# Context's first feed-forward chunk in full fp32, drawn between the steps of the lead's second product

## The chip, the cores and the metric

The kernel runs on one core of a Trainium2 chip. The metric is the device time of one execution in microseconds (us); lower is better. Times shown are medians of several runs; a profile is one execution recorded instruction by instruction. Engines are called PE (matmul), DVE (vector), ACT (scalar), POOL (GpSimd) and SP (the queue that issues most DMAs).

## The reference

One transformer layer is computed for 128 context tokens and 1024 latent tokens that share their weights: a feed-forward half-step, a mixer (attention and pooling), and a second feed-forward half-step, each with a residual, a layer norm and a modulation. The part that matters here is the first half-step:

```python
def _modulate(x, shift, scale):
    return x * (1.0 + scale) + shift

def _swiglu(h, w1, w2):
    a, b = jnp.split(h @ w1, 2, axis=-1)
    return (jax.nn.silu(a) * b) @ w2

f1 = _swiglu(_modulate(x, sh1, sc1), lw['ffn1_w1'], lw['ffn1_w2'])
x = _layer_norm(ALPHA * x + 0.5 * g1 * f1, lw['ln_g'][0], lw['ln_b'][0])
```

The model width is 1024 and the hidden width 2816. Shift and scale come from products of a condition vector with `w_mod`; context and latent tokens have conditions of their own.

## The kernel before, in words

**Numbers.** Most products are made of three matmuls each (`mm3`, lines 130 to 132): both operands are split into a high and a low part of type fp32r, the high one by a copy on ACT (line 107), the low one by a subtraction on DVE (line 108), and high x high, high x low and low x high are added up in PSUM. `wide` makes such a pair of a weight and `parted` one of an x piece. A plain fp32 matmul needs no split; the kernel uses it for the modulation products of line 224, for the spread of line 169 and for small transposes (line 232).

**The first block's opening.** `ffn` calls `lead` and then `up`. In `lead` the modulation is made chunk by chunk (`mod_head`, of eight chunks; five by PE on line 224, three by DVE on line 214, whose products go into scratch tiles of the `tmp` tag). As soon as chunk kc is there, the latent rows of piece 0 are loaded and modulated (`piece_input`, lines 416 and 417, on ACT at line 402) and split. The latent product is done in the manner of Strassen and Winograd with seven products, A11, A12, S1, S2, S4, S3 and A22, each of four matmul groups per weight pair. The lead does these for four pairs p at once: A11 as chunks 0 to 3 arrive; copies of it into `s1` (line 655); A12 for pairs 0 and 1 as chunks 4 to 7 arrive, then for pairs 2 and 3 (`second`, which adds on line 667 and takes a silu on line 668); then S1, whose weights are differences (`first_sum`, line 711) and whose operands are sums of the two x halves (`sum_operands`, line 457); then the rest, whose operands `next_operand` and `last_operands` make (lines 462 to 473, 738, 752 and 756).

**Context.** `ctx_ffn` is a generator that does the feed-forward of the 128 context tokens in six chunks of the hidden width, five of 512 and one of 256. A chunk of the up product takes 8 weights of 512 KB, each in two steps (value and gate half), then one step for the silu and product, one for transposes, and two for each of the four (at the end two) weights of the down product. Its first half-steps need the modulated context input, `ctx_x`, made from `x_c` in four loads. The generator is drawn by `tick(n)`, n steps at a time. In the first block it is added after the lead, and `up_prod` ticks once after each product of the 18 later pairs, and once more at A12 for pairs below 15 and at S2.

**What sets the order.** The order written is a priority. Before the run a planner that simulates the engines lists each engine's instructions in a fixed order: the ready one of highest priority first, and a tile's buffer is one of those that the pool has free. On the chip each engine, and SP's queue of DMA issues, takes its list strictly in that order. Pools that matter here: `raw`, five buffers of 4 KB a partition, into which SP loads weights (line 111); `tmp`, six buffers of 2 KB; `pc`, twelve of 2 KB; and eight PSUM banks.

Of the kernel before, what the change touches and what calls it, by code (L numbers as in the profile page):

```python
# [26 lines left out]
F32R = mybir.dt.float32r  # L27
# [5 lines left out]
P = 128  # L33
D = 1024
KC = 8
# [12 lines left out]
LAT, CTX = 0, 1  # L48
# [6 lines left out]
class Layer:  # L55
# [417 lines left out]
        self.A["A22"].append(self.parted(r, "b2", 12))  # L473


    def ctx_operands(self):
        place = self.xm if "xm" in self.pools else self.pc
        self.xc = [(place(F32R), place(F32R)) for _ in range(2)]

    def ctx_x(self, x, i, kcs):  # L480
        for kc in kcs:
            m = self.pc()[:, :P]
            self.modulated(m, x[kc], i, CTX, kc)
            ks = slice(kc % 4 * P, (kc % 4 + 1) * P)
            self.split(self.xc[kc // 4][0][:, ks], self.xc[kc // 4][1][:, ks], m)

    def ctx_x_dram(self):
        self.ctx_operands()
        for h in range(2):
            m = self.raw(self.x2_d[0][:, h * 512 : (h + 1) * 512], 512)  # L490
            b = self.bank()
            js = [slice(j * P, (j + 1) * P) for j in range(4)]
            for j in js:
                self.transpose(b[:, j], m[:, j])
            for k, j in enumerate(js):
                self.modulated(m[:, j], b[:, j], 2, CTX, 4 * h + k)
            self.split(self.xc[h][0], self.xc[h][1], m)
            yield

    def ctx_up(self, b, w, kc, n):  # L500
        hi, lo = self.wide(self.raw(w, 2 * n), 2 * n)
        ks = slice(kc % 4 * P, (kc % 4 + 1) * P)
        xh, xl = self.xc[kc // 4]
        for s in range(2):
            ns = slice(s * n, (s + 1) * n)
            self.mm3(b[s][:, :n], (xh[:, ks], xl[:, ks]), (hi[:, ns], lo[:, ns]), kc == 0, kc == KC - 1)
            yield

    def ctx_ffn(self, i, x, w1c, w1t, w2):
        nc = self.nc  # L510
        if x:
            self.ctx_operands()
            x()
        yield
        acc = None
        for c in range(6):
            n = 256 if c == 5 else 512
            banks = [self.bank(), self.bank()]
            for kc in range(KC):
                yield from self.ctx_up(banks, w1t[kc] if c == 5 else w1c[c, kc], kc, n)  # L520
            h = self.tmp() if c == 0 and "xm" in self.pools else self.pc()
            nc.scalar.activation(h[:, :n], banks[0][:, :n], AF.Silu)
            nc.vector.tensor_tensor(h[:, :n], h[:, :n], banks[1][:, :n], ALU.mult)
            yield
            if acc is None:
                acc = [self.bank(), self.bank()]
            b = self.bank()
            for j in range(n // P):
                self.transpose(b[:, j * P : (j + 1) * P], h[:, j * P : (j + 1) * P])
            hh, hl = self.pc(F32R), self.pc(F32R)  # L530
            self.split(hh[:, :n], hl[:, :n], b[:, :n])
            yield
            for j in range(n // P):
                f = 4 * c + j
                js = slice(j * P, (j + 1) * P)
                hi, lo = self.wide(self.raw(w2[f]))
                for d in range(2):
                    ds = slice(d * 512, (d + 1) * 512)
                    self.mm3(acc[d], (hh[:, js], hl[:, js]), (hi[:, ds], lo[:, ds]), f == 0, f == NF - 1)
                    yield  # L540
        for d in range(2):
            o = self.pc()
            nc.scalar.activation(o, acc[d], AF.Copy)
            nc.gpsimd.dma_start(self.fc_d[i][:, d * 512 : (d + 1) * 512], o)
            yield
# [34 lines left out]
    def up_pair(self, m, w1, h_d):  # L580

        nc = self.nc
        add, sub = (partial(nc.vector.tensor_tensor, op=o) for o in (ALU.add, ALU.subtract))
        halves = lambda t: (t[:, :512], t[:, 512:])
        ra, rb = self.raw(w1[2 * m]), self.raw(w1[2 * m + 1])
        (b11, b21), (b12, b22) = halves(ra), halves(rb)
        hi, lo = self.wide(ra)
        Y = self.bank()
        self.up_prod(Y, "A11", (hi[:, :512], lo[:, :512]), True)
        s1 = self.tmp()  # L590
        nc.scalar.activation(s1, Y, AF.Copy)
        yield
        t = self.tsum()
        sub(t[:, 0, :], b12, b11)
        sub(t[:, 1, :], b22, t[:, 0, :])
        t12 = self.wide(self.flat(t))
        Z = self.bank()
        self.up_prod(Z, "A12", (hi[:, 512:], lo[:, 512:]), True, 1 + self.spare * (m < 15))
        add(s1, Z, s1)
        nc.scalar.activation(s1, s1, AF.Silu)  # L600
        yield
        w22 = self.wide(b22, 512)
        X = self.bank()
        self.up_prod(X, "S1", [halves(w)[0] for w in t12], True)
        s5 = self.tmp()
        nc.scalar.activation(s5, X, AF.Copy)
        yield
        sub(b11, t[:, 1, :], b11)
        sub(b21, b21, t[:, 1, :])
        t34 = self.wide(ra)  # L610
        self.up_prod(Y, "S2", [halves(w)[1] for w in t12], False, 1 + self.spare)
        u2 = self.tmp()
        nc.scalar.activation(u2, Y, AF.Copy)
        yield
        self.up_prod(X, "S4", w22, False)
        add(u2, X, u2)
        nc.vector.tensor_tensor(u2, u2, s1, ALU.mult)
        self.keep_h(m, 0, u2, h_d)
        yield
        self.up_prod(Y, "S3", [halves(w)[0] for w in t34], False)  # L620
        add(s5, Y, s5)
        yield
        self.up_prod(Y, "A22", [halves(w)[1] for w in t34], False)
        sa = self.tmp()
        nc.scalar.activation(sa, Y, AF.Silu)
        nc.vector.tensor_tensor(s5, s5, sa, ALU.mult)  # L626
        self.keep_h(m, 1, s5, h_d)
        self.h_sums(m, u2, s5, h_d)
        yield
# [20 lines left out]
    def lead(self, w1, h_d, piece, make, Y=None):  # L650


        nc = self.nc
# [18 lines left out]
        if not begun:  # L672
# [9 lines left out]
            s1 = [self.tmp() for p in R]  # L682
            for p in R:
                copy(s1[p], Y[p])
            Z = [self.bank() for p in range(2)]
            for k in range(4):
                if k < 3:
                    ready(5 + k)
                if k >= 2:
                    S += [self.sum_operands(piece, j) for j in (2 * k - 4, 2 * k - 3)]  # L690
                for p in range(2):
                    self.up_unit(Z[p], "A12", W2[p], k, k == 0, k == 3)
            for p in R:
                second(p, Z[p] if p < 2 else self.bank(), p >= 2)
        else:
            W2 = [self.wide(part(0, p, 1), 512) for p in R]
            s1 = [self.tmp() for p in R]
# [32 lines left out]
        else:  # L730
            for p in R:
                first_sum(p)
                X.append(self.bank())
                prod(X[p], "S1", self.wide(T[p], 512), True)
                self.next_operand(p, *S[p])
        for p in R:
            r = part(1, p, 1)
# [12 lines left out]
        for p in R:  # L750
            r = part(0, p, 0)
            sub(r, T[p], r)
            prod(Y[p], "S3", self.wide(r, 512), False)
            add(s5[p], Y[p], s5[p])
            r = part(0, p, 1)
            sub(r, r, T[p])
            prod(Y[p], "A22", self.wide(r, 512), False)
            sa = self.tmp()
            nc.scalar.activation(sa, Y[p], AF.Silu)
            nc.vector.tensor_tensor(s5[p], s5[p], sa, ALU.mult)  # L760
            self.keep_h(p, 1, s5[p], h_d)
            if begun and p == 0:
                self.tick(5)

    def up(self, w1, h_d):
# [220 lines left out]
    def ffn(self, i, head, res_of, dst, order, half, beside=None, begun=None):  # L986
# [3 lines left out]
        with ExitStack() as st:  # L990
# [10 lines left out]
                self.begin_operands()  # L1001
            piece, make, ctx_x, mods = head()
            context = self.ctx_ffn(i // 2, ctx_x, a["w1c_" + s], a["w1t_" + s], a["w2_" + s])
            if begun:
                self.add_side(context)
            self.lead(a["w1_" + s], h_d, piece, make, Y)
            self.mods = mods
            if not begun:
                self.add_side(context)
            self.up(a["w1_" + s], h_d)  # L1010
            self.flush()
            for _ in self.mods:
# [8 lines left out]

    def head_input(self):
        nc, a = self.nc, self.a

        def ctx_x():
            for q in range(4):
                x = self.pc()
                nc.sync.dma_start(x[:, :256], a["x_c"][q])
                self.ctx_x({q: x[:, :P], q + 4: x[:, P:256]}, 0, (q, q + 4))

        def mods():
            for part in range(2, 5):
                yield from self.mod_part(part)
# [10 lines left out]
            if kc == 0:  # L1044
                self.spread(1, rows[2:])

        return self.piece_input, make, ctx_x, mods()

    def head_dram(self):
        return self.piece_dram, lambda kc: None, None, self.mod_part(8)  # L1050
# [536 lines left out]
def _layout(inputs):  # L1587
# [32 lines left out]
    for i, w in enumerate(WINDOWS):  # L1620
# [3 lines left out]
    return {  # L1624
        "x": con(x),
        "x_l": con(x[P:].T.reshape(KC, P, 2, 512).transpose(2, 0, 1, 3)[::-1]),
        "x_c": con(x[:P].T.reshape(2, 4, P, P).transpose(1, 2, 0, 3)).reshape(4, P, 256),
        "w_mod": con(wm_t[16:]),
        "w_mod_v": con(np.stack([np.stack([wm_t[k], wm_t[KC + k]]) for k in DVE_KC])),
        "w_mod_h": con(  # L1630
# [53 lines left out]
```

## Time and profile before

| what | value |
|---|---|
| median of 3 runs | 2496.45 us (2493.36 to 2497.18) |
| the profiled execution, its own time | 2495.49 us |
| span of the profile | 2493.7 us |
| PE busy | 2452.3 us, 98% of the span |
| DVE busy | 1830.6 us, 73% |
| ACT busy | 1214.5 us, 49% |
| moved by DMA | 463.75 MB, mean 186 GB/s |

A profile's row of a group reads: line, engine, operation, output tile and input tiles, partitions by elements and type, how many times, then busy time and mean ns of one, then the idle time of the engine just before and what released it. A row of the order in time begins with the start and the length in us; `x4` means four instructions merged into one row. The ends of matmuls are modelled and overlap with the next start, so the distance from one start to the next is what one costs. In a view of stretches each engine has its busy us with the number of instructions behind it, and then come the granted PE clock as a share of full speed, the share of DMA time and GB/s.

The lead lies in the first 125 us or so; the up stage follows until about 557 us, where the context's result is stored.

### The profile page before, as it was taken

The page shows a single profiled execution, that of the slowest core. Times are in us where ns is not written, and L with a number is a line of the kernel's source. Part 1 is how long each engine was busy: PE and PEld are TensorE (multiplying, and loading weights), DVE is VectorE, ACT ScalarE, POOL GpSimd, SP SyncE. Part 2 cuts the span into 40 slices and gives each one's busy share as a digit, 9 for nine tenths or more (in the row PEclk, how much of TensorE's full clock was granted, in tenths as well). Part 3 has the DMA queues.
Part 4 walks back from the last instruction along what each step waited for, and adds up shares of the span by engine and source line. Part 5 has one row for each costly group of instructions (what it writes and reads, how often), then busy time and mean ns, then how long its engine had stood idle before and what let it go on. Part 6 is the DMA issues. An engine that isn't in the chain of part 4 may idle for free.

```text
span 2493.7 us, 34226 instructions
## 1 busy us (share of the span) xinstructions
PE 2452.3 (98%) x12297; PEld 2115.0 (85%) x12297; DVE 1830.6 (73%) x2817; ACT 1214.5 (49%) x2094; POOL 463.4 (19%) x691
## 2 busy tenths in 40 slices
PE   8999999999999999999999999999899999999998
PEld 4788888888889989889999999998688888887887
DVE  6877778877678556566888886876877666676877
ACT  5544444444445343434778773435744344444442
POOL 0000011110022212232567640110000001111002
PEclk9999999999999999999999999999999999999999
DMA  7455566778686555534100035665754445558773
GB/s 292 144 167 188 182 224 230 244 259 326 213 276 218 184 180 189 188 136 163 42 1 2 1 110 187 237 215 185 223 173 164 150 173 195 205 197 320 269 267 121
DMA packets 167554, 463.75 MB, mean 186 GB/s; under 512 B 18900, under 2 KB 37636, under 8 KB 167384
## 3 DMA queue, kind: packets, MB, share of 16 engines
q1 hardware_dynamic: 140952, 373.79, 44.7%
q0 software_dynamic: 23696, 86.32, 9.3%
q8 instruction: 97, 1.59, 0.3%
q10 hardware_dynamic: 2736, 1.44, 0.2%
q14 instruction: 73, 0.60, 0.1%
HBM read 390.42 MB, written 71.07 MB: 185 GB/s over the span
## 4 chain that ended last, share of the span: by engine, by line
PE 84%; DVE 6%; issue 4%; DMA 3%; ACT 2%; POOL 1%; SPq 0%; DVEq 0%; POOLq 0%; ACTq 0%
PE w L130 24%; PE w L131 24%; PE w L132 24%; PE w L1060 8%; PE w L135 3%; DVE op L108 1%; DVE x L108 1%; DMA raw<-w 1%; DVE mx L1389 1%; PE w L224 0%; DMA yc<-fc 0%; ACT pr L1397 0%; DMA raw<-w1c 0%; DVE so L108 0%; DMA raw<-x 0%
## 5 line engine op out<-in xcount | busy, mean ns | idle before, releaser
L107 ACT ACTIVATE op<-raw 128x1024 fp32r<-128x1024 f32 (+1 forms) x505 | 483.9, 969 | 517.4 <-PE w L131 263.4
L108 DVE TENSOR_TENSOR op<-raw,op 128x1024 fp32r<-128x1024 f32 (+1 forms) x505 | 558.9, 1116 | 233.1 <-ACT op L107 201.1
L130 PE MATMUL w<-b,op 128*128 128x512 f32 x880 | 343.9, 393 | 7.1 <-ACT b L107 2.9
L131 PE MATMUL w<-b,op 128*128 128x512 f32 x880 | 344.6, 392 | 0.0
L132 PE MATMUL w<-b,op 128*128 128x512 f32 x880 | 339.7, 391 | 0.3 <-DVE op L108 0.3
L130 PE MATMUL w<-x,op 128*128 128x384 f32 x768 | 260.0, 339 | 0.0
L131 PE MATMUL w<-x,op 128*128 128x384 f32 x768 | 258.8, 337 | 0.0
L132 PE MATMUL w<-x,op 128*128 128x384 f32 x768 | 257.7, 337 | 0.0
L131 PE MATMUL w<-op,so 128*128 128x512 f32 (+1 forms) x627 | 242.4, 387 | 2.0 <-DVE op L108 2.0
L132 PE MATMUL w<-op,so 128*128 128x512 f32 (+1 forms) x627 | 241.9, 387 | 0.0
L130 PE MATMUL w<-op,so 128*128 128x512 f32 (+1 forms) x627 | 232.7, 386 | 1.0 <-ACT op L107 0.9
L130 PEld LDWEIGHTS w<-b,op 128*128 128x128 f32 x880 | 165.6, 188 | 42.9 <-ACT b L107 3.4
L562 POOL DMA_DIRECT2D h<-tmp x80 | 43.4, 543 | 851.6 <-DVE tmp L626 426.1
L132 PEld LDWEIGHTS w<-b,op 128*128 128x128 f32 x880 | 165.8, 188 | 35.8 <-DVE op L108 0.8
L131 PEld LDWEIGHTS w<-b,op 128*128 128x128 f32 x880 | 165.8, 188 | 34.8 <-DVE b L108 0.7
L1402 POOL TENSOR_TENSOR pr<-pr,sm 128x384 f32<-128x384 f32 x192 | 156.1, 842 | 95.1 <-DVE sm L1400 71.8
L190 DVE SCALAR_TENSOR_TENSOR junk<-raw,sil 128x1024 bf16<-128x1024 f32 x112 | 135.9, 1224 | 26.0 <-DMA raw<-w_mod 25.6
L107 ACT ACTIVATE so<-sr 128x1024 fp32r<-128x1024 f32 (+1 forms) x84 | 82.7, 986 | 136.1 <-PE w L131 82.7
L131 PEld LDWEIGHTS w<-x,op 128*128 128x128 f32 x768 | 144.1, 188 | 0.3
L130 PEld LDWEIGHTS w<-x,op 128*128 128x128 f32 x768 | 144.1, 188 | 0.4
L132 PEld LDWEIGHTS w<-x,op 128*128 128x128 f32 x768 | 143.9, 188 | 0.0
L131 PEld LDWEIGHTS w<-op,so 128*128 128x128 f32 x627 | 118.2, 189 | 26.8 <-DVE op L108 3.2
(323 smaller groups left out, 5136.6 us busy)
## 6 DMA issues: line engine op xcount, KB each, us to landing
raw<-w SPq DMA_DIRECT2D x240, 256.0 KB, 5.3
raw<-w SPq DMA_DIRECT2D x116, 512.0 KB, 3.9
raw<-w1c SPq DMA_DIRECT2D x80, 512.0 KB, 4.0
sr<-h SPq DMA_DIRECT2D x70, 512.0 KB, 5.7
raw<-w_mod SPq DMA_DIRECT2D x56, 512.0 KB, 4.3
raw<-w_gate SPq DMA_DIRECT2D x48, 512.0 KB, 3.7
h<-tmp POOLq DMA_DIRECT2D x80, 256.0 KB, 3.6
h<-pc POOLq DMA_DIRECT2D x52, 256.0 KB, 4.6
```

Source lines behind the costliest of these rows:

```text
L107: self.nc.scalar.activation(hi, src, AF.Copy)
L108: self.nc.vector.tensor_tensor(lo, src, hi.bitcast(F32), ALU.subtract)
L130: mm(out, lhsT=lh, rhs=rh, start=start, stop=False)
L131: mm(out, lhsT=lh, rhs=rl, start=False, stop=False)
L132: mm(out, lhsT=ll, rhs=rh, start=False, stop=stop)
L135: self.nc.tensor.transpose(out, src, self.ident)
L190: nc.vector.scalar_tensor_tensor(junk, w, 1.0, self.sil[cond], ALU.mult, ALU.mult, accum_out=self.mod[:, cond, b : b + 1],)
L562: self.nc.gpsimd.dma_start(h_d[f // 2][:, 2 * kh + n, f % 2, :], h)
L1060: self.nc.tensor.matmul(acc[h][j], lhsT=lhs[:, part, js], rhs=w[wi][:, h * 512 : (h + 1) * 512], start=f, stop=l)
L1389: nc.vector.tensor_reduce(mx[:, c : c + 1], b[:, :GT], AX.X, ALU.max)
L1402: nc.gpsimd.tensor_tensor(pr[:, c, :], pr[:, c, :], sm[:, 3:4].broadcast_to([P, GT]), ALU.mult)
```

## The change

In the first block the context generator is added before the lead, and the lead draws it. Chunk 0 of its up product no longer uses split operands: `ctx_whole_input` loads all of the context input into two `tmp` tiles with one tick ahead of A12; each weight's two steps then modulate one 128x128 part of it in place and do one plain fp32 matmul each, straight from the loaded weight. Four such steps follow each of the four matmul groups of A12 for pair 0. A12 of pairs 1 to 3 comes whole afterwards, each followed by the `sum_operands` of one index, which came earlier before. The S1 weights are split for all four pairs ahead of the S1 products, with one tick (the silu of chunk 0) between. Five ticks now also come at A22 of pair 0 in the first block. Chunk 1 and later chunks use the split context input as before; it is made at chunk 1's start from a second load of `x_c` (`ctx_parts_input`). The extra ticks in `up_prod` become fewer. `x_c` lies in memory as two blocks of 512 columns and no longer as four of 256. The second block's work is the same as before.

```diff
+    def ctx_whole_input(self):
+        self.xf = [self.tmp() for _ in range(2)]
+        for h, x in enumerate(self.xf):
+            self.nc.sync.dma_start(x, self.a["x_c"][h])
+
+    def ctx_parts_input(self):
+        self.xc = [(self.pc(F32R), self.pc(F32R)) for _ in range(2)]
+        for h in range(2):
+            m = self.pc()
+            self.nc.sync.dma_start(m, self.a["x_c"][h])
+            for k in range(4):
+                js = slice(k * P, (k + 1) * P)
+                self.modulated(m[:, js], m[:, js], 0, CTX, 4 * h + k)
+            self.split(self.xc[h][0], self.xc[h][1], m)
...
-    def ctx_up(self, b, w, kc, n):
+    def ctx_up(self, b, w, kc, n, whole):
+        ks = slice(kc % 4 * P, (kc % 4 + 1) * P)
+        if whole:
+            x = self.xf[kc // 4][:, ks]
+            self.modulated(x, x, 0, CTX, kc)
+            r = self.raw(w, 2 * n)
+            for s in range(2):
+                self.nc.tensor.matmul(
+                    b[s][:, :n], lhsT=x, rhs=r[:, s * n : (s + 1) * n],
+                    start=kc == 0, stop=kc == KC - 1,
+                )
+                yield
+            return
         hi, lo = self.wide(self.raw(w, 2 * n), 2 * n)
...
             banks = [self.bank(), self.bank()]
+            if x and c == 1:
+                x[1]()
             for kc in range(KC):
-                yield from self.ctx_up(banks, w1t[kc] if c == 5 else w1c[c, kc], kc, n)
+                yield from self.ctx_up(banks, w1t[kc] if c == 5 else w1c[c, kc], kc, n, x and c == 0)
-            h = self.tmp() if c == 0 and "xm" in self.pools else self.pc()
+            h = self.tmp() if c == 0 else self.pc()
...
-        self.up_prod(Z, "A12", (hi[:, 512:], lo[:, 512:]), True, 1 + self.spare * (m < 15))
+        self.up_prod(Z, "A12", (hi[:, 512:], lo[:, 512:]), True, 1 + self.spare * (m < 10))
...
-        self.up_prod(Y, "S2", [halves(w)[1] for w in t12], False, 1 + self.spare)
+        self.up_prod(Y, "S2", [halves(w)[1] for w in t12], False)
...
-            Z = [self.bank() for p in range(2)]
+            Z = self.bank()
             for k in range(4):
                 if k < 3:
                     ready(5 + k)
-                if k >= 2:
-                    S += [self.sum_operands(piece, j) for j in (2 * k - 4, 2 * k - 3)]
-                for p in range(2):
-                    self.up_unit(Z[p], "A12", W2[p], k, k == 0, k == 3)
+                if k == 0:
+                    self.tick(1)
+                self.up_unit(Z, "A12", W2[0], k, k == 0, k == 3)
+                self.tick(4)
             for p in R:
-                second(p, Z[p] if p < 2 else self.bank(), p >= 2)
+                second(p, self.bank() if p else Z, p > 0)
+                S.append(self.sum_operands(piece, p))
...
             for p in R:
                 first_sum(p)
+            W = [self.wide(T[p], 512) for p in R]
+            self.tick(1)
+            for p in R:
                 X.append(self.bank())
-                prod(X[p], "S1", self.wide(T[p], 512), True)
+                prod(X[p], "S1", W[p], True)
                 self.next_operand(p, *S[p])
...
-            if begun and p == 0:
+            if p == 0:
                 self.tick(5)
...
-            if begun:
-                self.add_side(context)
+            self.add_side(context)
             self.lead(a["w1_" + s], h_d, piece, make, Y)
             self.mods = mods
-            if not begun:
-                self.add_side(context)
```

More of the change, by code (lines that the diff above doesn't have):

```diff
@@ L473, in last_operands @@
         self.A["A22"].append(self.parted(r, "b2", 12))
[L476 to L485, printed above, removed]
+    def ctx_whole_input(self):
[11 more added lines that the diff above has]
+            self.split(self.xc[h][0], self.xc[h][1], m)
     def ctx_x_dram(self):
-        self.ctx_operands()
+        self.xc = [(self.xm(F32R), self.xm(F32R)) for _ in range(2)]
         for h in range(2):
@@ L498, in ctx_x_dram @@
             yield
-    def ctx_up(self, b, w, kc, n):
+    def ctx_up(self, b, w, kc, n, whole):
[11 more added lines that the diff above has]
+            return
         hi, lo = self.wide(self.raw(w, 2 * n), 2 * n)
-        ks = slice(kc % 4 * P, (kc % 4 + 1) * P)
         xh, xl = self.xc[kc // 4]
@@ L511, in ctx_ffn @@
         if x:
-            self.ctx_operands()
-            x()
+            x[0]()
         yield
@@ L1023, in head_input @@
         nc, a = self.nc, self.a
[L1025 to L1029, printed above, removed]
         def mods():
@@ L1045, in make @@
                 self.spread(1, rows[2:])
-        return self.piece_input, make, ctx_x, mods()
+        return self.piece_input, make, (self.ctx_whole_input, self.ctx_parts_input), mods()
     def head_dram(self):
@@ L1626, in _layout @@
         "x_l": con(x[P:].T.reshape(KC, P, 2, 512).transpose(2, 0, 1, 3)[::-1]),
-        "x_c": con(x[:P].T.reshape(2, 4, P, P).transpose(1, 2, 0, 3)).reshape(4, P, 256),
+        "x_c": con(x[:P].T.reshape(2, 4, P, P).transpose(0, 2, 1, 3)).reshape(2, P, 512),
         "w_mod": con(wm_t[16:]),
```

## The prediction

> **What bounds the kernel now.** I read the page's totals first, then the stretches of the opening and of the up stage, then the TensorE (PE) instructions in order of time.
>
> ```profile
> span 2493.7 us, 34226 instructions
> PE 2452.3 (98%) x12297; PEld 2115.0 (85%) x12297; DVE 1830.6 (73%) x2817; ACT 1214.5 (49%) x2094; POOL 463.4 (19%) x691
> ```
>
> ```profile
> 40.00:45.00 5.00, 5.00 (x24) 3.34 (x23) 2.21 (x8) 3.79 (x7) 0.00 (x0) 1.00 1.05 386
> 45.00:50.00 5.00, 4.73 (x22) 2.28 (x21) 5.00 (x16) 5.00 (x9) 0.00 (x0) 1.00 0.53 195
> ...
> 100.00:150.00 50.00, 50.00 (x222) 41.39 (x222) 33.34 (x45) 17.59 (x23) 3.78 (x7) 1.00 0.46 156
> ```
>
> ```profile
> 50.00:55.00 5.00, 4.79 (x21) 3.63 (x21) 4.81 (x9) 5.00 (x10) 0.00 (x0) 1.00 0.35 107
> 55.00:60.00 5.00, 3.79 (x17) 2.81 (x16) 5.00 (x10) 3.55 (x7) 0.00 (x0) 1.00 0.35 105
> 60.00:65.00 5.00, 1.39 (x4) 0.37 (x2) 5.00 (x10) 1.30 (x3) 0.00 (x0) 0.84 0.17 54
> 65.00:70.00 5.00, 4.48 (x11) 3.52 (x12) 5.00 (x9) 4.40 (x8) 0.00 (x0) 0.50 0.36 103
> 70.00:75.00 5.00, 5.00 (x23) 4.14 (x22) 5.00 (x10) 5.00 (x11) 0.00 (x0) 0.97 0.17 57
> ```
>
> The columns are PE, weight load, DVE, ACT, POOL, granted clock, DMA share and GB/s. From 100 us on PE is full, so there time is the count of matmuls. From 45 to 70 us PE has a hole while DVE is full, and after it the granted clock is 0.50. The hole's size comes from the matmuls themselves:
>
> ```profile
> 42.47 0.28 PE L232 MATMUL w<-ident,ts 2*128 2x2 f32 x2
> ...
> 44.27 3.62 PE L224 MATMUL w<-wm,silt 128*2 128x256 f32 x16
> ...
> 58.30 0.50 PE L131 MATMUL w<-ax,op 128*128 128x512 f32 x1 [1.21 <-DVE ax L108]
> ...
> 60.02 0.39 PE L132 MATMUL w<-ax,op 128*128 128x512 f32 x1
> 62.03 0.50 PE L130 MATMUL w<-b,op 128*128 128x512 f32 x1 [1.62 <-ACT op L107]
> 62.51 0.49 PE L131 MATMUL w<-b,op 128*128 128x512 f32 x1
> 65.52 0.79 PE L130 MATMUL w<-b,op 128*128 128x512 f32 x1 [2.52 <-DVE tmp L667]
> ...
> 70.33 0.40 PE L132 MATMUL w<-b,op 128*128 128x512 f32 x1
> 70.57 0.39 PE L130 MATMUL w<-b,op 128*128 128x512 f32 x1
> ...
> 91.89 0.39 PE L130 MATMUL w<-b,op 128*128 128x512 f32 x1
> ```
>
> From 70.57 to 91.89 94 matmuls start: 0.227 us each. From 42.47 to 70.57 (28.1 us) PE runs the 48 matmuls of the second product (A12, four pairs), the modulation product L224 of chunk 7, two small transposes, and 14 matmuls of S1. At full pace that is 62 x 0.227 + 3.6 + 0.4 = 18.1 us, so the hole is 10.0 us: about 4.8 us of waiting between 60.25 and 65.52, 2.3 us because 12 matmuls took 5.05 us at the low clock instead of 2.7, and 3 us in small gaps.
>
> **The change, part by part.** *Removed.* Context's chunk 0 no longer splits its weights; 16 steps of three matmuls leave the full up stage: 48 x 0.227 = **-10.9 us**, one for one, as PE is full there. The eight ACT copies and eight DVE subtractions that go with them were covered by that PE work and count nothing; if a step had waited for its pair it would gain more, but a stretch with 50.00 of 50.00 shows no such wait.
>
> *Added.* 16 full fp32 matmuls, 128x128 by 128x512, among the A12 of pair 0. The trace has none of that size; the nearest rows:
>
> ```profile
> L224 PE MATMUL w<-wm,silt 128*2 128x256 f32 x80 | 22.5, 445 | 0.2 <-DMA wm<-w_mod_h 0.2
> ```
>
> ```profile
> 14.15 0.18 PEld L169 LDWEIGHTS w<-pc,ones 1*128 1x128 f32 x1 [0.24 <-issue]
> 14.58 0.18 PEld L169 LDWEIGHTS w<-pc,ones 1*128 1x128 f32 x1 [0.24 <-issue]
> ```
>
> Each fp32 matmul is two PE instructions (eight written in L224 for one chunk, x16 in the row at 44.27). There 16 passes of 256 columns take 3.62 us, 0.226 each, so 0.45 for 512; the 512-column passes of L169 load 0.43 apart. A step is 0.86 to 0.91 us; I take 0.88, between two near ends: **+14.1 us** (13.8 to 14.5).
>
> *Where that lands.* Hole 10.0 us, fill 14.1: if the steps fill it, S1, which now runs as if from 70.57 - 14 x 0.227 = 67.4 us without a break, starts at 42.47 + 10.9 + 3.6 + 0.4 + 14.1 = 71.5. The lead is 4.1 us longer, and the whole is 4.1 - 10.9 = **-6.8 us** before new stalls. The steps need no split, so they depend only on DMA and on a 128x128 modulation each (eight; ACT):
>
> ```profile
> L402 ACT ACTIVATE pc<-pc,md 128x128 f32<-128x128 f32 x8 | 3.8, 488 | 3.9 <-DMA pc<-x_c 3.9
> ...
> L711 DVE TENSOR_TENSOR ts<-raw 128x512 f32<-128x512 f32 x4 | 2.7, 684 | 0.0
> ```
>
> Eight of 0.49 us are 3.9 us on ACT, in place of eight 512-wide modulations of the second x piece that come later; nothing on PE waits for them but the steps.
>
> *DMA and SP's queue.* Eight loads of 512 KB and two of 256 KB (4.7 MB) now stand ahead of these:
>
> ```profile
> 28.47 0.33 SPq L416 DMA_DIRECT2D xp<-x_l  x1
> 29.75 8.81 SPq L416 DMA_DIRECT2D pc<-x_l  x8
> 38.90 32.92 SPq L111 DMA_DIRECT2D raw<-w  x17
> ```
>
> ```profile
> pc<-x_l SPq DMA_DIRECT2D x12, 256.0 KB, 8.2
> ```
>
> At 386 GB/s they take 12.2 us. The eight pieces of x's second half, landed by about 46 now (the last issue at 29.75 + 8.81 - 0.33 = 38.2, and 8.2 to land), land by 59. The raw pool has five buffers, so the sixth to eighth weight must wait on SP until PE finished steps 2, 4 and 6 (about 46 to 53 us), with x and the first_sum halves queued behind: first pair by 51 to 56, last by 59 to 61. DVE still owes S1 four adds, four splits, four subtractions L711, four splits of these and four L667: 20 x 0.69 = 13.8 us, from about 56 to 70, against S1 at 71.5. That fits with little to spare. The stall has ends of 0 (all ordered well) and 9 us (next part); the margin is on the lower end's side, and I take **2 us**: -4.8 us.
>
> What such a stall costs depends on the clock. The gap of 1.21 us at 58.30 was followed by matmuls at the full pace; the stretch from 60.25 to 65.52, with two matmuls in it, by 12 at half, at 2.3 us. A stall of 2 us lies between these, nearer to the first, so I add nothing; with the drop the sum is -2.5. The Trainium skill ("TensorE: Matmul & The Clock Gate", section "What's actually happening") states that the clock halves after an idle window of about 3.4 us. This trace agrees on both sides, 1.21 and 4.8 us; by it a 2 us stall stays free of the drop and the sum is -4.8 too.
>
> *Costed at nothing.* The number of steps drawn stays 155: before 18 x 7 + 11 + 18, after 1 + 16 + 1 + 5 in the lead and 18 x 7 + 6, so nothing piles up in the flush. The later x_c load and its eight modulations and two splits at chunk 1 (8 x 0.49 + 2 x 0.69 = 5.3 us of ACT and DVE) lie under the full PE; if a step of chunk 1 had to wait for them, that is the price. The five ticks put two weight splits into the lead, on DVE, after S1.
>
> **The rivals.** *DVE's run only moves back.* Its order is fixed before the run; what S1 needs may again stand behind the S2 and S4 operands.
>
> ```profile
> 45.41 0.69 DVE L457 TENSOR_TENSOR pc<-pc,pc 128x512 f32<-128x512 f32 x1
> ...
> 64.78 2.48 DVE L667 TENSOR_TENSOR tmp<-w,tmp 128x512 f32<-128x512 f32 x4
> ```
>
> Now S1 comes 67.4 - 45.4 = 22 us after the first add. From a first add at 56 that makes 78; with 2.3 us of low clock, 80.5: a stall of 9 us and a net of +2.2: 2498.6. For it speaks that L667 ran at 64.78 although the products ended by 60.4. Against it: the adds of the second half now stand behind L667 in the order written, and fewer can be ahead of it.
>
> *Slower: the six tmp buffers.* Four hold s1 and two the context input, so none is left for chunk 6's products on DVE, whose scratch has the same tag.
>
> ```profile
> 41.22 2.07 ACT L655 ACTIVATE tmp<-w 128x512 f32<-128x512 f32 x4 [3.03 <-PE w L132]
> ```
>
> ```profile
> 37.31 1.22 DVE L214 SCALAR_TENSOR_TENSOR junk<-wm,sil 128x1024 bf16<-128x1024 f32 x1
> ...
> 43.06 1.22 DVE L214 SCALAR_TENSOR_TENSOR junk<-wm,sil 128x1024 bf16<-128x1024 f32 x1
> ...
> 46.09 1.22 DVE L214 SCALAR_TENSOR_TENSOR junk<-wm,sil 128x1024 bf16<-128x1024 f32 x1
> ```
>
> If they wait for the first input half, freed after step 8 (42.5 + 3.6 + 6 x 0.227 + 8 x 0.88 = 54.5), DVE stands in its queue till then, four products take 4.9 us, and A12's third part starts at about 62. If DVE's 22 us then begin, S1 starts at 84: a stall of 12.5 us, +5.7: 2502. It decides from a stall of 11.8 us. Against it: the first of the four ran ahead of the copies at 37.31, and the steps that remain can run meanwhile.
>
> *More gain.* No stall at all, and fewer steps per pair ease DVE in the up stage. PE's idle time there is about 1 us, so -6.8 becomes about -8: 2488.5.
>
> That the steps run in one block and are not spread changes PE's sum by nothing; it is in the first two cases.
>
> **How the numbers follow.** The profiled execution took 2495.49 us around its span of 2493.7; the median of the runs is 2496.45, 1 us above. The differences are taken from the median. A measurement here tells 0.2%, 5 us, from no change. Forecast, stall 0 to 4 us (-6.8 to -2.8): 0.50, at -4.8 = **2491.6**. DVE's run moved back: 0.22. Tmp buffers: 0.16. More gain: 0.12. The forecast is under -5 for stalls below 1.8 us, 0.30 of its 0.50. Faster 0.30 + 0.12 = 0.42; same 0.20 + 0.22 = 0.42; slower 0.16. The range reaches from the last case's far side to the tmp case: 2487 to 2502.5; the forecast's own is 2489.6 to 2493.7.
>
> **What would show it.** The step as pairs of fp32 passes at 0.43 to 0.455 us; PE without a gap over 2 us between 42 and 72 and the clock at 1.00 there; S1 from 71 to 74 us; 48 fewer matmuls with pc operands in the up stage, whose end comes 3 to 7 us earlier. It would be wrong if S1 starts after 78, if junk or x_l on the queues waits for a buffer past 55, or if the up stage does not shrink by about 11 us.

## The result, and the profile after

The changed kernel takes 2509.74 us in the median of 6 runs (2506.03 to 2510.59), against 2495.96 us for 6 runs of the kernel before (2493.36 to 2497.18). The ratio is 1.0054, 95% interval 1.0043 to 1.0064: slower by 13.8 us. The forecast was 2491.6, with a range up to 2502.5.

The profiled execution is longer by 11.8 us of span. From the page of the changed kernel:

```profile
span 2505.5 us, 34175 instructions
PE 2458.9 (98%) x12281; PEld 2113.4 (84%) x12281; DVE 1822.6 (73%) x2803; ACT 1208.7 (48%) x2088; POOL 461.9 (18%) x691
```

The context's sum is read back for the first norm at 642.4 us before and 654.7 us after, 12.3 us later; from there to the end the distance stays between 10 and 12.5 us (11.8 at the same read-back of the second block). So all of it is lost ahead of that, and the stretches of the opening show where (columns as in the prediction: PE, weight load, DVE, ACT, POOL, granted clock, DMA share, GB/s):

```profile
45.00:50.00 5.00, 0.73 (x2) 0.30 (x2) 3.53 (x7) 4.69 (x8) 0.00 (x0) 0.61 0.85 333
50.00:55.00 5.00, 3.40 (x4) 1.17 (x4) 2.40 (x4) 2.94 (x7) 0.00 (x0) 0.50 0.01 4
55.00:60.00 5.00, 5.00 (x19) 1.80 (x19) 0.00 (x0) 0.37 (x1) 0.00 (x0) 0.87 0.30 105
60.00:65.00 5.00, 5.00 (x13) 2.14 (x12) 0.16 (x1) 0.00 (x0) 0.00 (x0) 1.00 0.47 137
...
70.00:75.00 5.00, 1.62 (x6) 1.05 (x6) 5.00 (x15) 3.98 (x7) 0.00 (x0) 1.00 0.73 238
75.00:80.00 5.00, 3.42 (x5) 1.52 (x6) 5.00 (x10) 5.00 (x10) 0.00 (x0) 0.68 0.61 194
80.00:85.00 5.00, 5.00 (x18) 3.16 (x17) 5.00 (x10) 0.67 (x2) 0.00 (x0) 0.98 0.64 207
```

PE stands still at 45 to 51 and again after 68, and DVE, which was full here before, does nothing from 55 to 64 us. The PE instructions in order of time (L511 is the fp32 step):

```profile
42.25 0.28 PE L232 MATMUL w<-ident,ts 2*128 2x2 f32 x2
...
45.54 0.40 PE L132 MATMUL w<-ax,op 128*128 128x512 f32 x1
51.60 3.78 PE L511 MATMUL w<-raw,tmp 128*128 128x512 f32 x4 [5.67 <-ACT tmp L402]
55.31 4.09 PE L224 MATMUL w<-wm,silt 128*2 128x256 f32 x16
59.33 8.85 PE L511 MATMUL w<-raw,tmp 128*128 128x512 f32 x20
68.11 0.28 PE L232 MATMUL w<-ident,ts 2*128 2x2 f32 x2
71.83 0.47 PE L130 MATMUL w<-ax,op 128*128 128x512 f32 x1 [3.44 <-DVE md L202]
72.14 0.40 PE L131 MATMUL w<-ax,op 128*128 128x512 f32 x1
72.38 0.39 PE L132 MATMUL w<-ax,op 128*128 128x512 f32 x1
...
73.07 0.39 PE L132 MATMUL w<-ax,op 128*128 128x512 f32 x1
76.58 1.07 PE L130 MATMUL w<-ax,op 128*128 128x512 f32 x2 [3.13 <-ACT ax L107]
77.49 5.03 PE L511 MATMUL w<-raw,tmp 128*128 128x512 f32 x8
81.95 0.80 PE L131 MATMUL w<-ax,op 128*128 128x512 f32 x1
82.59 0.39 PE L132 MATMUL w<-ax,op 128*128 128x512 f32 x1
```

A pass is one of the two PE instructions of an fp32 matmul. Twenty passes start within 59.33 to 68.0: 0.434 us each, 0.87 a step, as the prediction had it. From 42.25 to 82.59 (40.3 us; PE is full after it) the work is 15 A12 matmuls x 0.227, 32 passes x 0.434, 3.6 for L224 and 0.4 for the small transposes: 21.3 us. The hole is 19.0 us, where it was 10.0. With the 16 steps at +13.9 and the 48 matmuls at -10.9 the sum is +3.0 + 9.0 = +12.0, against 11.8 in the spans. The price of the work was right; the hole doubled instead of closing.

Two other engines tell what PE waited for. SP's queue:

```profile
30.40 9.44 SPq L416 DMA_DIRECT2D pc<-x_l  x8
40.19 2.37 SPq L111 DMA_DIRECT2D raw<-w1c  x4
42.91 1.00 SPq L479 DMA_DIRECT2D tmp<-x_c  x2
55.41 7.97 SPq L111 DMA_DIRECT2D raw<-w1c  x3
64.78 60.44 SPq L111 DMA_DIRECT2D raw<-w  x27
```

and DVE:

```profile
51.74 0.69 DVE L108 TENSOR_TENSOR b<-xp,b 128x512 fp32r<-128x512 f32 x1
64.84 1.22 DVE L214 SCALAR_TENSOR_TENSOR junk<-wm,sil 128x1024 bf16<-128x1024 f32 x1 [12.41 <-issue]
```

The context input x_c is issued at 42.91, behind all of x's second half and five of the weights (one went ahead at 23.31), though its tick is written ahead of them; so the first step can't start before 51.60. And DVE waits 12.4 us in front of chunk 6's scratch. The row names no releaser. But that scratch and the context input share the `tmp` tag, and the scratch started at 64.84, when step 8, the last reader of the input's first half, was done (four passes by 55.3 and twelve from 59.33: 59.33 + 12 x 0.434 = 64.5).

### The profile page after: what moved, and what is told of

Read it like the earlier page. It is cut to its first block, busy times and chain, and to the rows that moved or that the text cites. A ratio compares the mean times of both kernels' runs of the same rounds, so it can differ in the third digit from the quotient of the medians.

```text
span 2505.5 us, 34175 instructions
## 1 busy us (share of the span) xinstructions
PE 2458.9 (98%) x12281; PEld 2113.4 (84%) x12281; DVE 1822.6 (73%) x2803; ACT 1208.7 (48%) x2088; POOL 461.9 (18%) x691
## 4 chain that ended last, share of the span: by engine, by line
PE 90%; DVE 5%; ACT 2%; DMA 2%; issue 1%; POOL 0%; SPq 0%; DVEq 0%; POOLq 0%; ACTq 0%
PE w L130 26%; PE w L131 26%; PE w L132 26%; PE w L1071 8%; PE w L135 3%; DMA raw<-w 1%; PE w L224 1%; DVE x L108 1%; DVE op L108 1%; DVE mx L1400 1%; PE w L511 1%; ACT pr L1408 0%; ACT pc L402 0%; DVE pl L1333 0%; ACT b L107 0%
## 5 line engine op out<-in xcount | busy, mean ns | idle before, releaser
L107 ACT ACTIVATE op<-raw 128x1024 fp32r<-128x1024 f32 (+1 forms) x497 | 475.0, 967 | 523.6 <-PE w L131 266.9
L108 DVE TENSOR_TENSOR op<-raw,op 128x1024 fp32r<-128x1024 f32 (+1 forms) x497 | 548.6, 1113 | 220.3 <-ACT op L107 182.5
L107 ACT ACTIVATE so<-sr 128x1024 fp32r<-128x1024 f32 (+1 forms) x84 | 82.7, 986 | 136.9 <-PE w L131 70.4
L130 PE MATMUL w<-ax,op 128*128 128x512 f32 x352 | 138.2, 399 | 9.1 <-ACT ax L107 5.7
```

Of the source, the lines that this page charges most:

```text
L107: self.nc.scalar.activation(hi, src, AF.Copy)
L108: self.nc.vector.tensor_tensor(lo, src, hi.bitcast(F32), ALU.subtract)
L130: mm(out, lhsT=lh, rhs=rh, start=start, stop=False)
```

## The experiments

In the tables of a trace some lines move by one where an edit adds a line; the fp32 step is then L512, the latent modulation L403.

**The two waits, one at a time and together.** `xf_mid` loads the context input earlier:

```diff
                     W2 = [self.wide(part(0, p, 1), 512) for p in R]
+                    self.tick(1)
                 for p in R:
...
-                if k == 0:
-                    self.tick(1)
                 self.up_unit(Z, "A12", W2[0], k, k == 0, k == 3)
```

> The changed kernel, with the one tick that loads the context input moved into the A11 loop (at chunk 2, behind the second weights). The two tmp tiles are then taken before the scratch of chunk 4, and x_c is loaded before the second half of x. Theory 'tmp buffers': two waits make up the loss, the late x_c (PE idle from 45.9 to 51.6 us, then half clock) and chunk 6's scratch waiting for step 8. This run takes away the first only: about 8 us less than the changed kernel, so +3 to +6 us against before. Rival 'queue' (eight 512 KB weights ahead of x's second half and of the first_sum halves on SP): stays at +10 to +14. Rival 'order of DVE' (the sums now late): stays at +10 to +14.

`junk_ts` moves chunk 6's scratch on DVE from `tmp` to the `ts` pool:

```diff
             for part in range(2):
+                wide = self.pools["ts"].tile([P, 2, D], BF16, tag="ts", name=self.name("junk"), bufs=2) if kc == 6 else None
...
-                    junk = self.junk()
+                    junk = self.junk() if wide is None else wide[:, cond, :]
```

> The changed kernel, with chunk 6's scratch on DVE in the ts pool and no longer in tmp. Theory 'tmp buffers': takes away the second wait only (DVE idle from 52.4 to 64.8 us); x_c stays late. PE's waits at 68.1 and 73.3 us go, some 6 to 9 us: +3 to +6 us against before. Rivals 'queue' and 'order of DVE': +9 to +14, as nothing on SP or in the order written has moved.

Both edits:

> Both edits: the early x_c and the scratch in ts. Theory 'tmp buffers': the forecast of the prediction comes about, -3 to -7 us against before. Rival 'queue': +5 or more, since all eight weights still stand ahead of the first_sum halves. Rival 'order of DVE': +3 or more.

And another way to the same end, the input in one buffer of the b2 pool:

```diff
-        self.xf = [self.tmp() for _ in range(2)]
+        t = self.pools["b2"].tile([P, D], F32, tag="b2", name=self.name("xf"), bufs=12)
+        self.xf = [t[:, :512], t[:, 512:]]
```

> The changed kernel, with the whole context input in one buffer of the b2 pool and no longer in two of tmp; the scratch stays in tmp and finds buffers there. Theory 'tmp buffers': the same as both edits together, -3 to -7 us against before, in another way. Rivals 'queue' and 'order of DVE': +3 or more.

Measured, all against the same runs of the kernel before (2495.05 us):

| kernel | median us | ratio, 95% interval | difference us |
|---|---|---|---|
| x_c early | 2496.59 | 1.0006 (0.9996 to 1.0015) | +1.5 |
| scratch in ts | 2506.35 | 1.0043 (1.0028 to 1.0058) | +11.3 |
| both | 2488.61 | 0.9976 (0.9967 to 0.9986) | -6.4 |
| input in b2 | 2489.47 | 0.9975 (0.9964 to 0.9985) | -5.6 |

The kernels without either wait come out faster than the one before, in two ways. That settles it for `tmp`: in both, all eight weights still stand ahead of the first_sum halves, and the sums stand where the new order writes them (with both edits they run from 46.8 to 54.3), so the rivals "queue" (the weights hold up x's second half and the first_sum halves on SP) and "order of DVE" (the sums now stand later) fall as first causes. PE in the kernel with both edits:

```profile
40.67 0.28 PE L233 MATMUL w<-ident,ts 2*128 2x2 f32 x2
40.88 0.50 PE L130 MATMUL w<-ax,op 128*128 128x512 f32 x1
41.22 1.88 PE L512 MATMUL w<-raw,tmp 128*128 128x512 f32 x4
...
51.58 7.03 PE L512 MATMUL w<-raw,tmp 128*128 128x512 f32 x16
58.04 1.03 PE L130 MATMUL w<-ax,op 128*128 128x512 f32 x2
58.91 1.88 PE L512 MATMUL w<-raw,tmp 128*128 128x512 f32 x4
...
61.55 3.60 PE L512 MATMUL w<-raw,tmp 128*128 128x512 f32 x8
...
70.44 0.39 PE L130 MATMUL w<-b,op 128*128 128x512 f32 x1
70.66 0.39 PE L131 MATMUL w<-b,op 128*128 128x512 f32 x1
71.79 0.50 PE L132 MATMUL w<-b,op 128*128 128x512 f32 x1 [0.74 <-DVE op L108]
72.13 0.40 PE L130 MATMUL w<-b,op 128*128 128x512 f32 x1
```

The steps begin at 41.22, S1 at 70.44. From 40.67 to 72.13 (31.5 us) lie 48 A12 and 3 S1 matmuls, 32 passes, L225 and the transposes: 29.5 us, a hole of 2.0. So +3.0 + 2.0 - 10.0 = -5.0, within the interval of the -6.4 measured.

The halves don't add up, and the expectations for them missed: the early load alone gave back 12 us and not 8, the scratch alone only 2, and its +11.3 lies in the range that the two rivals had for it. With x_c early but the scratch in `tmp`, DVE's wait shows its releaser:

```profile
53.69 0.68 DVE L108 TENSOR_TENSOR b<-xp,b 128x512 fp32r<-128x512 f32 x1
57.00 1.22 DVE L214 SCALAR_TENSOR_TENSOR junk<-wm,sil 128x1024 bf16<-128x1024 f32 x1 [2.63 <-PE w L511]
```

It is the fp32 step. PE of the same kernel (the first four passes lie at 42.64):

```profile
51.65 8.74 PE L511 MATMUL w<-raw,tmp 128*128 128x512 f32 x20
63.22 1.22 PE L130 MATMUL w<-ax,op 128*128 128x512 f32 x2 [2.83 <-ACT ax L107]
```

Step 8 is done at 51.65 + 12 x 0.434 = 56.9 and not at 64.5, so DVE's wait has shrunk from 12.4 to 2.6 us; PE still waits 2.8 us for the modulation that follows, and its clock is at half from 63.0 to 69.8. From 42.09 to 70.96, where PE is full again, lie 28.9 us for 21.3 us of work, a hole of 7.6: +3.0 + 7.6 - 10.0 = +0.6, for +1.5 measured.

With x_c late and the scratch out of the way, something else ends at nearly the same time. DVE of `junk_ts`, and then its SP queue:

```profile
53.66 1.28 DVE L469 TENSOR_TENSOR xp<-xp,pc 128x512 f32<-128x512 f32 x2
71.53 0.69 DVE L729 TENSOR_TENSOR ts<-raw 128x512 f32<-128x512 f32 x1 [16.59 <-DMA raw<-w]
```

```profile
42.94 1.00 SPq L480 DMA_DIRECT2D tmp<-x_c  x2
56.24 8.61 SPq L111 DMA_DIRECT2D raw<-w1c  x3
66.24 28.23 SPq L111 DMA_DIRECT2D raw<-w  x17
```

DVE now stands 16.6 us before the first_sum subtraction, whose halves SP issues only behind the last context weights. Those wait for one of the five raw buffers, and the buffers hold weights that no step has read, because the steps wait for x_c. So the rival "queue" was right about a wait, but as something that follows from the late x_c. The hole of this kernel (40.80 to 89.61 us, with 29.7 us of work) is 19.1 us, as large as that of the changed kernel. The late x_c thus reaches DVE in two ways, and taking away one leaves the other.

**Why x_c comes late.** The input in the b2 pool, with its tick where it was, settles that the pool held it back, and not the tick's place in the order written or SP's queue. Its issues (ns shortest/median/longest, first and last start in us):

```profile
L480 SPq DMA_DIRECT2D xf<-x_c x2: 327/328/328, 23.2 to 23.9; - x2
```

In `tmp`, the tick is written behind chunk 4's scratch and the four copies s1. Two kernels take these out of its way, first the scratch alone (the edit of `junk_ts` with `kc == 4`):

> What makes x_c late? The changed kernel with only chunk 4's scratch moved from tmp to ts; the tick stays behind the copies s1. If x_c waits in tmp for the tiles written ahead of it (chunk 4's scratch and s1), taking away the scratch alone leaves it behind s1: x_c is issued at about 43 us as before and the time stays at +9 to +14 us against the kernel before. If the scratch alone held it, x_c comes at about 24 us and the time is +1 to +4.

then also the copies:

```diff
+            self.tick(1)
             s1 = [self.tmp() for p in R]
...
-                if k == 0:
-                    self.tick(1)
```

> The changed kernel with chunk 4's scratch in ts and the tick written just ahead of the copies s1, so that nothing that comes late stands ahead of the context input in tmp. If x_c waits for the tiles written ahead of it, it is now issued at about 24 us, between chunk 5's and chunk 6's loads, and the time is that of the early x_c alone, +1 to +4 us against the kernel before; chunk 6's scratch still waits for step 8. If something else on SP held x_c (the full DMA queue, the weights), it stays at 40 us or later and the loss stays at +9 to +14.

The issues of x_c, of `junk4_ts` and then of `early_j4`:

```profile
L480 SPq DMA_DIRECT2D tmp<-x_c x2: 328/328/328, 43.0 to 43.7; - x2
```

```profile
L480 SPq DMA_DIRECT2D tmp<-x_c x2: 328/328/328, 23.3 to 24.0; - x2
```

The times go with them: 2510.07 us, ratio 1.0058 (1.0034 to 1.0082), and 2497.73 us, ratio 1.0008 (0.9997 to 1.0019), against 2495.52. So x_c moves by 20 us with the tiles written ahead of it in its pool, and the loss with it. In `junk4_ts` no tile of `tmp` is in use between chunk 1's scratch, done by 20 us, and the copies from 39.8 on; x_c waits all the same. The reading that fits all three kernels is that a tile gets its buffer only after those of the same tag that are written before it; it is inferred, no row of a trace says it.

**The rest of the change by itself.** First the price of fp32, chunk 0 at its old place (the diff is cut to the step):

```diff
...
+        if whole:
+            r = self.raw(w, 2 * n)
+            for s in range(2):
+                self.nc.tensor.matmul(
+                    b[s][:, :n], lhsT=self.xf[kc], rhs=r[:, s * n : (s + 1) * n],
+                    start=kc == 0, stop=kc == KC - 1,
+                )
+                yield
+            return
         hi, lo = self.wide(self.raw(w, 2 * n), 2 * n)
...
```

> The kernel before, with context's chunk 0 as 16 full fp32 matmuls at its old place after the lead; order, ticks and loads as before. It measures the price of fp32 by itself: PE is full there, 16 x 0.87 - 48 x 0.227 = +3.0 us, so +2 to +4 us. If the split's ACT and DVE work had held PE up in the up stage, the time would be unchanged or lower.

2497.84 us against 2494.59: ratio 1.0010 (1.0001 to 1.0019), +3.2 us where +3.0 was worked out. Its instructions:

```profile
L505 PE MATMUL w<-raw,pc 128*128 128x512 f32 x32 | 15.2, 591 | 0.0
L505 PEld LDWEIGHTS w<-raw,pc 128*128 128x128 f32 x32 | 6.0, 188 | 4.1 <-issue 3.4
```

Sixteen steps are 32 instructions; PE never waited ahead of one, and a load takes 188 ns, well under a pass. Here, where PE is full, full fp32 costs what its passes cost, and the split it saves on ACT and DVE buys nothing.

Then the lead's order (diff cut to its core):

```diff
-            Z = [self.bank() for p in range(2)]
+            Z = self.bank()
...
             for p in R:
-                second(p, Z[p] if p < 2 else self.bank(), p >= 2)
+                second(p, self.bank() if p else Z, p > 0)
+                S.append(self.sum_operands(piece, p))
...
+            W = [self.wide(T[p], 512) for p in R]
```

> The kernel before, with the lead's new order alone: A12 of one pair with the modulation, the other three after it, each followed by its sum, all S1 weights split ahead of S1; context and ticks as before. Theory 'tmp buffers': the order is no part of the loss, -2 to +2 us. Rival 'order of DVE': the late sums cost +3 us or more by themselves.

2494.82 us against 2494.59, ratio 1.0001 (0.9992 to 1.0010): nothing. Last, two kernels with the input in b2: one has the ticks of the up stage as they were (diff below, beside the edit of `xf_b2`), the other chunk 6's scratch in ts as well:

```diff
-        self.up_prod(Z, "A12", (hi[:, 512:], lo[:, 512:]), True, 1 + self.spare * (m < 10))
+        self.up_prod(Z, "A12", (hi[:, 512:], lo[:, 512:]), True, 1 + self.spare * (m < 15))
...
-        self.up_prod(Y, "S2", [halves(w)[1] for w in t12], False)
+        self.up_prod(Y, "S2", [halves(w)[1] for w in t12], False, 1 + self.spare)
```

> The context input in b2, and the extra ticks of the up stage as in the kernel before (11 + 18 and no longer 6), so that context ends earlier in the up stage. If fewer steps per pair relieve the up stage, as the case 'more gain' had it, this is slower than the run with the input in b2 alone by 1 us or more; I expect the same within 1.5 us: -4 to -7 against before.

> The context input in b2 and chunk 6's scratch in ts, so that tmp holds neither. Theory 'tmp buffers': with the input out of tmp the scratch finds buffers anyway, so nothing is added: -5 to -8 us against before, like the two other kernels without the waits.

They take 2489.20 us, ratio 0.9977 (0.9968 to 0.9986), and 2488.84 us, ratio 0.9976 (0.9966 to 0.9985), against 2494.59. Neither differs from the input in b2 alone. So the fewer ticks are worth nothing that these runs can tell, and the scratch needs no place of its own once the input is out of `tmp`. The change with its input in another pool beats the kernel before by 0.24%, a little under 6 us.

## Why the prediction was wrong, step by step

**Removed, added.** -10.9 and +14.1 us hold: a pass took 0.434 us (0.43 to 0.455 forecast), so the second is +13.9, `fp32_only` measured their sum at +3.2, and 48 matmuls with pc operands are gone, 16 on each of three lines (168 before):

```profile
L131 PE MATMUL w<-op,pc 128*128 128x512 f32 x152 | 59.2, 389 | 0.0
```

**Where that lands.** This is the step that failed. It said that the steps "depend only on DMA and on a 128x128 modulation", and took x_c to come where its tick is written. The steps depended on a buffer first. With x_c at 23 us and the scratch elsewhere the step comes out as it was written: S1 at 70.4 for 71.5, a hole of 2.0 us for the stall of 2 assumed, -6.4 and -5.6 us for -4.8. In the changed kernel two signs of being wrong came, the scratch after 55 (64.84) and S1 after 78 (87.35), and context's result is stored 10.1 us later (567.0 for 556.9) in place of 3 to 7 earlier.

**DMA and SP's queue.** Half wrong. x's second half did not wait behind the weights: all eight pieces were issued by 39.84, ahead of seven of them and of x_c. What did wait was what I gave less weight, the first_sum halves, from 38.90 before to 64.78, as the weights kept the raw buffers.

**The stall and the clock.** Instead of 2 us the hole holds a wait of 5.8 us (45.8 to 51.6), one of 3.5 and one of 3.3, and two spells at half clock: 7.7 us for 5.4 us of work from 51.60, 6.0 us for 4.2 us of work from 76.58. These five make 16.8 of the 19.0. The trace of the kernel before was also read too simply: the 4.8 us between 60.25 and 65.52 are no idle window but gaps of 1.8 and 2.8 us with two matmuls between, and cut into stretches of 0.2 us the granted clock falls at 63.4, only 0.7 us into the second gap. So this trace did not show that a stall of 2 us is free of the drop.

**The rivals.** The tmp buffers were named as the slower case, with the right tiles, the right step that frees them and the right engine standing still, at a chance of 0.16 and +5.7 us. The price was too low, because the same count of buffers was applied to the scratch alone: step 8 was put at 54.5, with x_c there from the start; it ended at 64.5. S1, put at 84 in that case, runs as if from 90.1 without a break (82.59 + 33 x 0.227). What was said against the case, that "the first of the four ran ahead of the copies at 37.31", held for the old order only; in the new one the input's two tiles stand ahead of it, and none of the four ran before 64.84. "DVE's run only moves back" did not occur in the kernels without the waits, and the order alone measured nothing; its price counted the low clock twice, as the 22 us to 67.4 already hold the 2.3 (without them S1 at 78, a stall of 6.5 and -0.3 us). "More gain" through fewer ticks measured nothing either.

**Costed at nothing.** The context's later input and the five ticks are also in the kernels at -6 us, which are no slower than the sum without them (-5.0): no cost shows.

## What to carry to other kernels

When work is moved ahead in time, list for each tile that it takes which tiles of the same pool are written before it and when they get and give back their buffers; a load with no inputs is as late as its pool. A hole on the busiest engine is worth its length only to work whose operands can be there when it opens. Two waits that hide each other must be taken away together: alone they looked worth 12 and 2 us, and the two 20.

## What was not expected

A load without inputs was held back for 20 us by its pool while no tile in it was in use (x_c at 43.0 or at 23.3 us, by what was written ahead of it).

PE's clock did not go by the length of one gap. In the changed kernel the gap of 3.44 us ahead of 71.83 was followed by matmuls at the full pace (72.38 to 72.60), and the clock of 70 to 75 us is 1.00; a second gap, of 3.13 us by its row, ahead of 76.58, with only 1.5 us of work between, was followed by eight passes in 5.03 us and a clock of 0.68 for 75 to 80. The Trainium skill ("TensorE: Matmul & The Clock Gate", section "What's actually happening") states that the window of activity is about 3.4 us long and free-running. This trace agrees: in stretches of 0.2 us the granted clock falls at 46.1 us, rises at 56.3, falls at 76.8 and rises at 80.2, and the distances of 10.2, 20.5 and 3.4 us are 3, 6 and 1 times 3.41; in the kernel before, from the fall at 63.4 to the rise at 70.3, it is about 2 times. Nor was PE idle for a whole window ahead of a fall: five matmuls start in the 3.4 us before 46.1 (42.80 to 45.54), and the longest gap there is 1.05 us. How little work is too little, these traces do not say.
